# Masks of a top-128 selection read off the scores that sixteen rounds of replacement have taken out

## The chip, the cores and the metric

The kernel runs on one core of a Trainium2 chip. The metric is the device time of one execution in microseconds (us), median of three runs. Engines are named as the profile names them: PE (matrix products), PEld (its weight loads), DVE (VectorE), ACT (ScalarE), POOL (GpSimd), SP (the engine whose queue issues all transfers here, SPq in the rows). Each engine works through its own instructions in order and waits for semaphores of the others.

## The reference

One decoder layer on 512 tokens of width 1024: rmsnorm, one wide projection, two token mixers side by side, a gated merge, a feed-forward block, a last rmsnorm. The first mixer (A) is a mixture of dilated attentions. The second (B) is attention over selected keys, and the selection is what the change touches:

```python
def one_block(args):                      # 128 queries at a time
    causal = key_pos[None, :] <= q_pos[:, None]
    dots = jnp.einsum('bqhd,bsd->bqhs', qi_blk, ki)
    score = jnp.einsum('bqh,bqhs->bqs', wi_blk, jax.nn.relu(dots)) * IDX_SCALE
    score = jnp.where(causal[None], score, -jnp.inf)
    _, sel = lax.top_k(score, topk)       # topk = min(256, T // 4) = 128
    valid = sel <= q_pos[None, :, None]
    ...                                   # softmax over the selected keys only
    return jnp.einsum('bhqk,bqkd->bhqd', p, v_sel)
```

So each query of the blocks 1, 2 and 3 (the tokens from 128 on) attends to the 128 earlier tokens of the highest score; queries of block 0 have at most 128 and take all of them.

## The kernel before, in words

Tokens stand in four blocks of 128. All products are of float32 accuracy: each operand is split into a high and a low part (`whi`/`wlo` for weights, `hTh`/`hTl` for the normalised input), and `mm3` (lines 203 to 205) issues three products. Weights come through `Chunk`: a transfer into `raw` on the SP queue, a copy to `whi` on ACT (line 174), a subtraction to `wlo` on POOL (line 166).

Scores. Before 85 us the scores of mixer B stand in `score[3]`, `score[2]`, `score[1]`, of 512, 384 and 256 columns (one row a query); block 0 needs no selection. A POOL operation (line 872) fills the keys after the query with LOWEST = -3.0e38.

Selection. The generator `topk_ops` (from line 625) searches all three blocks side by side: sixteen times `max` gives the eight largest of each row (line 631), and `match_replace` writes LOWEST over these eight (line 636) in the copy `cur[b]`; after the sixteenth `max` no replacement is made. Then six operations a block turn the 128th value into a mask: count the ties at the threshold among the 128 (line 642), find the ties in the row (644), number them by a scan (646), keep as many as are needed (647), add all that are larger (648), and map 1 and 0 to 0 and -1e30 (649). All of it is on DVE. The mask lies in the tile of the scores, and mixer B's softmax adds it (line 680).

What runs beside it. From 77 us on, the attention of mixer A runs, one `attn_step` after another: score products (`sc`, line 615), softmax (`sm`: DVE line 680, ACT line 681, reciprocal on DVE line 685, scaling on POOL line 686), transposes (`pT`, line 695), split of the transposed probabilities (`pth` on ACT line 699, `ptl` on DVE line 700), value products (`y`, lines 709 to 712), their sum (`A1y`, line 716, with `low` on ACT line 714). Between the steps PE works off a queue of projections, among them `proj` for va (values of mixer A) and `slot` for queries, keys and gates. va is split as well: the high half on ACT (line 564), the low half on DVE (line 565), two tiles a product, and the product's PSUM tile (`acc`, three of them) is free after the second low half. A slot product for keys is copied out by ACT (`raw`, line 490), crossed by two transfers into `sw` (line 493), and rotated on DVE (`z`, lines 497, 500, 501), then split into `kBh` on ACT (458) and `kBl` on DVE (462).

What sets the order. PE's order is as written in the code (a manual schedule). The other engines' orders are made when the program is built, by a scheduler that picks by priority levels: attention at level 2, projections at level 3, the selection at level 4, last. Once built, each engine's order is fixed; an instruction that comes late holds back all behind it on its engine.

Of the kernel before, what the change touches and what calls it, by code (L numbers as in the profile page):

```python
# [11 lines left out]
F32 = mybir.dt.float32  # L12
F32R = mybir.dt.float32r
AF = mybir.ActivationFunctionType
ALU = mybir.AluOpType

P = 128
# [9 lines left out]
TOPK = 128  # L27
EPS = 1e-6
NEG = -1.0e30
LOWEST = -3.0e38  # L30
ATTN_SCALE = HD ** -0.5
IDX_SCALE = (64 ** -0.5) * (8 ** -0.5)

# [5 lines left out]
def hybrid_block(ctx: ExitStack, tc: tile.TileContext, x, norm_mix, w_in, w_up_a, w_up_b, w_out,  # L39
                 norm_ffn, w_gate, w_up, w_down, norm_final, c_rope, c_ropeT, c_mask, out):  # L40
    nc = tc.nc
# [7 lines left out]
    small = ctx.enter_context(tc.tile_pool(name="small", bufs=4))  # L49
    at_stack = ExitStack()  # L50
    wp = ctx.enter_context(tc.tile_pool(name="wp", bufs=1))
    ap = at_stack.enter_context(tc.tile_pool(name="ap", bufs=1))
# [14 lines left out]
    def k2(dt=F32, name="k2"):  # L67
        return kp.tile([P, 512], dt, tag="k2", bufs=K2, name=name)
# [287 lines left out]
    def fill(us):  # L356

        debt[0] += us
        with level(3):
            while queue and debt[0] > 0:  # L360
                run_part()
        if not queue:
            debt[0] = min(debt[0], 0.0)
# [245 lines left out]
    def qk_units(units, name):  # L609

        tiles = [sps(name) for _ in units]
        mms = [qk(t, q, k, half, b, (b + 1) * P) for t, (q, k, half, b) in zip(tiles, units)]
        for i in range(2):
            for m in mms:
                nc.tensor.matmul(*m[i], start=i == 0, stop=i == 1)
        return tiles
# [7 lines left out]
    top, cur = {}, {}  # L624

    def topk_ops():

        for r in range(TOPK // 8):
            for b in (3, 2, 1):
                src = score[b] if r == 0 else cur[b]  # L630
                yield nc.vector.max(top[b][:, 8 * r:8 * r + 8], src[:, :(b + 1) * P])
            if r < TOPK // 8 - 1:
                for b in (3, 2, 1):
                    w = (b + 1) * P
                    src = score[b] if r == 0 else cur[b]
                    yield nc.vector.match_replace(cur[b][:, :w], top[b][:, 8 * r:8 * r + 8], src[:, :w], LOWEST)
        for b in (3, 2, 1):
            w = (b + 1) * P
            thr = top[b][:, TOPK - 1:TOPK]
            need = small.tile([P, 1], F32, name="need")  # L640
            e0 = ap.tile([P, TOPK], F32, tag="e0", bufs=1, name="e0")
            yield nc.vector.tensor_scalar(e0, top[b], thr, None, op0=ALU.is_equal, op1=ALU.add, accum_out=need)
            eq = ap.tile([P, 512], F32, tag="eq", bufs=1, name="eq")[:, :w]
            yield nc.vector.tensor_scalar(eq, score[b][:, :w], thr, None, op0=ALU.is_equal)
            cs = cur[b][:, :w]
            yield nc.vector.tensor_tensor_scan(cs, eq, eq, 0.0, op0=ALU.add, op1=ALU.bypass)
            yield nc.vector.scalar_tensor_tensor(eq, cs, need, eq, op0=ALU.is_le, op1=ALU.mult)
            yield nc.vector.scalar_tensor_tensor(eq, score[b][:, :w], thr, eq, op0=ALU.is_gt, op1=ALU.add)
            yield nc.vector.tensor_scalar(score[b][:, :w], eq, 1.0, -NEG, op0=ALU.subtract, op1=ALU.mult)
            maskb[b] = score[b]  # L650

    topk = []
# [15 lines left out]
    class Head:  # L668
# [6 lines left out]
        def softmax(self, p_, b):  # L675
# [3 lines left out]
            st = small.tile([P, 3], F32, name="st", bufs=8)  # L679
            nc.vector.tensor_tensor_reduce(sm, p_[:, :w], self.mask(b), -ATTN_SCALE, 3.0e38, ALU.add, ALU.min, st[:, 0:1])  # L680
            nc.scalar.activation(sm, sm, AF.Exp, bias=st[:, 0:1], scale=-1.0, accum_out=st[:, 1:2])  # L681
# [172 lines left out]
    score = {}  # L854
    for b in (3, 2, 1):
        w = (b + 1) * P
        score[b] = sc = ap.tile([P, 512], F32, tag="score", bufs=3, name=f"score{b}")
        sp = k2(name="scorep") if PH[0] >= 0 else None
        for hp in range(4):
            for s, p_ in enumerate(qk_units([(idxT[1 + hp], idxT[0], s, b) for s in range(2)], "dots")):  # L860
                h = 2 * hp + s
                rl = ap.tile([P, 512], F32, tag="sm", bufs=4, name="relu")
                nc.scalar.activation(rl[:, :w], p_[:, :w], AF.Relu)
                eng, to = (nc.gpsimd, sp) if h in PH else (nc.vector, sc)
                if h == 0 or h == PH[0]:
                    eng.tensor_scalar(to[:, :w], rl[:, :w], wis[:, b, h:h + 1], 1.0, op0=ALU.mult, op1=ALU.mult)
                else:
                    eng.scalar_tensor_tensor(to[:, :w], rl[:, :w], wis[:, b, h:h + 1], to[:, :w], op0=ALU.mult, op1=ALU.add)
                if sp is not None and h == NH - 1:
                    nc.vector.tensor_tensor(sc[:, :w], sc[:, :w], sp[:, :w], op=ALU.add)  # L870
            fill(DOTF)
        nc.gpsimd.affine_select(out=sc[:, b * P:w], in_=sc[:, b * P:w], compare_op=ALU.is_ge, fill=LOWEST, base=0,
                                pattern=[[-1, P]], channel_multiplier=1)
    drain()
    for b in (3, 2, 1):
        top[b] = const.tile([P, TOPK], F32, name=f"top{b}")
        cur[b] = ap.tile([P, 512], F32, tag="cur", bufs=3, name=f"cur{b}")
    topk.append(topk_ops())

    PLO[0] = PLOA  # L880
# [149 lines left out]
    for f in range(0, NF, 2):  # L1030
# [14 lines left out]
        for j in range(2):  # L1045
# [11 lines left out]
            tag, bufs = (("y", YB) if i >= 2 else ("rp", 2) if i == 1 else ("k2", K2))  # L1057
# [141 lines left out]
def _constants():  # L1199
# [10 lines left out]
    n[d < 0] = 0  # L1210
    mask = np.where(n > 0, np.log(np.maximum(n, 1)) / ATTN_SCALE, NEG).astype(np.float32)
    return tab, tabT, mask
# [24 lines left out]
```

## Time and profile before

| what | before |
|---|---|
| median of three runs | 767.15 us (764.58 to 769.06) |
| the profiled execution | 764.99 us, of which the span from first to last instruction 763.2 |
| PE busy | 733.3 us, 96% of the span |
| DVE busy | 503.4 us, 66% |
| ACT busy | 378.4 us, 50% |
| POOL busy | 258.8 us, 34% |
| mean granted clock of PE | 0.991 |

How to read it: the time of a profiled execution is its span and a little around it. Shares are means over the whole span; a stage of 30 us can have another bound than the mean tells. A row of the trace gives the start (or, in groups, the sum), the duration, the engine, the line of the kernel, and in brackets how long the engine stood idle before it and who released it. PE's products overlap, so the distance between two starts says more than a duration.

### The profile page before, as it was taken

The numbers are of one execution on the slowest core, as the hardware profiler recorded it, in microseconds if no ns is written. First come the engines' busy times: TensorE is split into PE (matmuls) and PEld (weight loads), VectorE is DVE, ScalarE is ACT, GpSimd is POOL, SyncE is SP. The second block draws the span as 40 slices with busy tenths as digits, with TensorE's granted clock in tenths as the row PEclk, the third lists the DMA queues.
The fourth block names the chain that finished last, engine by engine and source line by source line (L and its number), as shares of the span: only waits on it lengthen the run. The fifth ranks groups of instructions, "written<-read, shape, count | busy, mean of one in ns | idle before, by whom it ended". The sixth has DMA issues, their size and how long they took to land.

```text
span 763.2 us, 10914 instructions
## 1 busy us (share of the span) xinstructions
PE 733.3 (96%) x3567; PEld 616.1 (81%) x3567; DVE 503.4 (66%) x1063; ACT 378.4 (50%) x771; POOL 258.8 (34%) x245
## 2 busy tenths in 40 slices
PE   8987998997999999999999999999999999999995
PEld 7976887886888888888887888888888888888874
DVE  5879998999757557848225444344454457877885
ACT  6366656665656666634246333333333334545553
POOL 1653567563554554523222222222222220000043
PEclk9999999999999999999999999999999999999999
DMA  7342243322342212443332343334433452756722
GB/s 266 96 124 70 67 120 91 95 65 70 84 126 70 69 57 69 141 137 105 100 85 69 103 131 110 104 105 131 131 105 104 130 179 84 230 171 212 248 84 110
DMA packets 76280, 88.70 MB, mean 116 GB/s; under 512 B 6256, under 2 KB 57600, under 8 KB 76224
## 3 DMA queue, kind: packets, MB, share of 16 engines
q1 hardware_dynamic: 76224, 88.02, 38.3%
q8 instruction: 28, 0.46, 0.2%
q14 instruction: 28, 0.23, 0.1%
HBM read 79.08 MB, written 5.64 MB: 111 GB/s over the span
## 4 chain that ended last, share of the span: by engine, by line
PE 79%; DVE 13%; ACT 3%; issue 3%; DMA 1%; POOL 1%; SPq 0%; DVEq 0%; ACTq 0%; POOLq 0%
PE u L204 5%; PE u L205 5%; PE u L203 5%; PE g L205 5%; PE g L204 5%; PE g L203 5%; PE o L205 4%; PE o L203 4%; PE o L204 4%; PE gate L203 3%; PE gate L204 3%; PE gate L205 3%; PE x L203 2%; PE x L205 2%; PE x L204 2%
## 5 line engine op out<-in xcount | busy, mean ns | idle before, releaser
L166 POOL TENSOR_TENSOR wlo<-raw,whi 128x512 fp32r<-128x512 f32 (+1 forms) x138 | 183.4, 1339 | 401.8 <-ACT whi L174 398.5
L174 ACT ACTIVATE whi<-raw 128x512 fp32r<-128x512 f32 (+1 forms) x206 | 126.7, 624 | 164.2 <-PE u L205 70.0
L166 DVE TENSOR_TENSOR wlo<-raw,whi 128x512 fp32r<-128x512 f32 x68 | 50.7, 746 | 67.6 <-ACT whi L174 67.1
L205 PE MATMUL g<-h2l,whi 128*128 128x512 f32 x176 | 68.7, 390 | 0.0
L203 PE MATMUL g<-h2h,whi 128*128 128x512 f32 x176 | 68.7, 390 | 0.0
L204 PE MATMUL g<-h2h,wlo 128*128 128x512 f32 x176 | 68.6, 390 | 0.0
L203 PE MATMUL u<-h2h,whi 128*128 128x512 f32 x176 | 68.5, 389 | 0.0
L204 PE MATMUL u<-h2h,wlo 128*128 128x512 f32 x176 | 68.5, 389 | 0.0
L205 PE MATMUL u<-h2l,whi 128*128 128x512 f32 x176 | 68.5, 389 | 0.0
L686 POOL TENSOR_SCALAR sm<-sm,st 128x256 f32<-128x256 f32 (+3 forms) x64 | 40.0, 632 | 60.1 <-DVE st L685 50.8
L203 PE MATMUL gate<-hTh,whi 128*128 128x512 f32 x128 | 51.6, 403 | 0.0
L205 PE MATMUL gate<-hTl,whi 128*128 128x512 f32 x128 | 50.2, 392 | 0.0
L204 PE MATMUL gate<-hTh,wlo 128*128 128x512 f32 x128 | 50.1, 392 | 0.0
L1050 DVE TENSOR_TENSOR u<-u,rb 128x512 f32<-128x512 f32 x22 | 15.2, 691 | 49.0 <-PE u L205 49.0
L681 ACT ACTIVATE sm<-sm,st 128x256 f32<-128x256 f32 (+3 forms) x64 | 35.6, 557 | 23.6 <-DVE st L680 23.5
L203 PE MATMUL slot<-hTh,whi 128*128 128x512 f32 x104 | 42.4, 407 | 1.8 <-DVE va L565 1.1
L203 PE MATMUL proj<-whi,hTh 128*128 128x256 f32 (+1 forms) x128 | 38.3, 301 | 3.7 <-DVE va L565 1.6
L205 PE MATMUL slot<-hTl,whi 128*128 128x512 f32 x104 | 41.6, 400 | 0.0
L204 PE MATMUL slot<-hTh,wlo 128*128 128x512 f32 x104 | 41.4, 398 | 0.0
L203 PEld LDWEIGHTS u<-h2h,whi 128*128 128x128 f32 x176 | 33.0, 188 | 6.9
L204 PEld LDWEIGHTS u<-h2h,wlo 128*128 128x128 f32 x176 | 33.0, 188 | 6.9
L204 PE MATMUL proj<-whi,hTl 128*128 128x256 f32 (+1 forms) x128 | 38.0, 297 | 0.6 <-DVE hTl L315 0.6
(351 smaller groups left out, 1849.1 us busy)
## 6 DMA issues: line engine op xcount, KB each, us to landing
raw<-in_w_in SPq DMA_DIRECT2D x54, 256.0 KB, 3.0
raw<-in_w_gate SPq DMA_DIRECT2D x44, 256.0 KB, 2.8
raw<-in_w_up SPq DMA_DIRECT2D x44, 256.0 KB, 2.9
raw<-in_w_down SPq DMA_DIRECT2D x43, 256.0 KB, 4.2
wraw<-in_w_down SPq DMA_DIRECT2D x28, 256.0 KB, 3.3
x<-in_x SPq DMA_DIRECT2D x16, 256.0 KB, 4.6
raw<-in_w_in SPq DMA_DIRECT2D x32, 128.0 KB, 2.6
raw<-in_w_out SPq DMA_DIRECT2D x16, 256.0 KB, 2.6
```

Of the source, the lines that this page charges most:

```text
L166: eng.tensor_tensor(lo, raw, hi.bitcast(F32), op=ALU.subtract)
L174: nc.scalar.activation(hi, raw, AF.Copy)
L203: nc.tensor.matmul(o, l[0], r[0], start=start, stop=False)
L204: nc.tensor.matmul(o, l[1], r[0], start=False, stop=False)
L205: nc.tensor.matmul(o, l[0], r[1], start=False, stop=stop)
L681: nc.scalar.activation(sm, sm, AF.Exp, bias=st[:, 0:1], scale=-1.0, accum_out=st[:, 1:2])
L686: nc.gpsimd.tensor_scalar(sm, sm, st[:, 2:3], 1.0, op0=ALU.mult, op1=ALU.mult)
L1050: nc.vector.tensor_tensor(u, p_, rb2, op=ALU.mult)
```

## The change

The sixteenth round replaces too, as the fifteen before it. After it every selected score in `cur[b]` is LOWEST and nothing else is, since the keys after the query are now filled with another constant, NEVER = -3.3e38. The mask is read off with one operation a block: not equal to LOWEST gives 1, times NEG = -1e30. The six operations a block and their tiles (`need`, `e0`, `eq`) go.

```diff
+NEVER = -3.3e38
...
-            if r < TOPK // 8 - 1:
-                for b in (3, 2, 1):
-                    w = (b + 1) * P
-                    src = score[b] if r == 0 else cur[b]
-                    yield nc.vector.match_replace(cur[b][:, :w], top[b][:, 8 * r:8 * r + 8], src[:, :w], LOWEST)
+            for b in (3, 2, 1):
+                w = (b + 1) * P
+                src = score[b] if r == 0 else cur[b]
+                yield nc.vector.match_replace(cur[b][:, :w], top[b][:, 8 * r:8 * r + 8], src[:, :w], LOWEST)
         for b in (3, 2, 1):
             w = (b + 1) * P
-            thr = top[b][:, TOPK - 1:TOPK]
-            need = small.tile([P, 1], F32, name="need")
-            e0 = ap.tile([P, TOPK], F32, tag="e0", bufs=1, name="e0")
-            yield nc.vector.tensor_scalar(e0, top[b], thr, None, op0=ALU.is_equal, op1=ALU.add, accum_out=need)
-            eq = ap.tile([P, 512], F32, tag="eq", bufs=1, name="eq")[:, :w]
-            yield nc.vector.tensor_scalar(eq, score[b][:, :w], thr, None, op0=ALU.is_equal)
-            cs = cur[b][:, :w]
-            yield nc.vector.tensor_tensor_scan(cs, eq, eq, 0.0, op0=ALU.add, op1=ALU.bypass)
-            yield nc.vector.scalar_tensor_tensor(eq, cs, need, eq, op0=ALU.is_le, op1=ALU.mult)
-            yield nc.vector.scalar_tensor_tensor(eq, score[b][:, :w], thr, eq, op0=ALU.is_gt, op1=ALU.add)
-            yield nc.vector.tensor_scalar(score[b][:, :w], eq, 1.0, -NEG, op0=ALU.subtract, op1=ALU.mult)
+            yield nc.vector.tensor_scalar(score[b][:, :w], cur[b][:, :w], LOWEST, NEG, op0=ALU.not_equal, op1=ALU.mult)
             maskb[b] = score[b]
...
-        nc.gpsimd.affine_select(out=sc[:, b * P:w], in_=sc[:, b * P:w], compare_op=ALU.is_ge, fill=LOWEST, base=0,
+        nc.gpsimd.affine_select(out=sc[:, b * P:w], in_=sc[:, b * P:w], compare_op=ALU.is_ge, fill=NEVER, base=0,
```

The instruction orders of PE, POOL and SP are the same in both programs. DVE's differs from the end of the sixteenth search to the next softmax but one, ACT's in the place of one va. Line numbers of the changed kernel are smaller by 10 from line 660 on (680 becomes 670), and larger by one before the selection. In the rows, cur_1085, cur_1087, cur_1089 and score_738, score_838, score_958 are the blocks 3, 2, 1.

DVE behind the sixteenth search, before:

```order
L642 TENSOR_SCALAR e_1231,need<-top_1084 128x128
L644 TENSOR_SCALAR eq<-score_738,top_1084 128x512
L680 ISA sm,st<-sc,lc 128x512
L680 ISA st 128x1
L680 ISA sm,st<-sc,lc 128x256
L680 ISA st 128x1
L700 TENSOR_TENSOR ptl<-pT,pth 128x128
L700 TENSOR_TENSOR ptl<-pT,pth 128x3x128
L685 RECIPROCAL st<-st 128x1
L646 SCALAR_TENSOR_TENSOR cur_1085<-eq 128x512
L685 RECIPROCAL st<-st 128x1
L642 TENSOR_SCALAR e_1240,need<-top_1086 128x128
```

and the same place now (from the first reciprocal on):

```order
L675 RECIPROCAL st<-st 128x1
L636 MATCH_REPLACE cur_1087<-top_1086,cur_1087 128x384
L675 RECIPROCAL st<-st 128x1
L636 MATCH_REPLACE cur_1089<-top_1088,cur_1089 128x256
L498 TENSOR_TENSOR z<-raw,ropeT 64x512
L639 TENSOR_SCALAR score_738<-cur_1085 128x512
L639 TENSOR_SCALAR score_838<-cur_1087 128x384
L639 TENSOR_SCALAR score_958<-cur_1089 128x256
L566 SCALAR_TENSOR_TENSOR va_2060<-proj,rs_147,va_2060 128x2x64
L566 SCALAR_TENSOR_TENSOR va_2063<-proj,rs_147,va_2063 128x2x64
```

What moved: of the old operations only three replacements and three masks are left, the masks now stand in one row, and the first two low halves of va follow right behind them.

DVE around the fourth low half of va (the second of va_2084, in the changed program va_2063), before:

```order
L462 TENSOR_TENSOR kBl<-z,kBh 64x512 x2
L685 RECIPROCAL st<-st 128x1 x2
L565 SCALAR_TENSOR_TENSOR va_2084<-proj,rs_147,va_2084 128x2x64
L716 TENSOR_TENSOR A1y<-y,low 64x512
L700 TENSOR_TENSOR ptl<-pT,pth 128x4x128
L700 TENSOR_TENSOR ptl<-pT,pth 128x2x128
L647 SCALAR_TENSOR_TENSOR eq<-cur_1087,need,eq 128x384
```

and now:

```order
L463 TENSOR_TENSOR kBl<-z,kBh 64x512 x2
L675 RECIPROCAL st<-st 128x1 x2
L566 SCALAR_TENSOR_TENSOR va_2060<-proj,rs_147,va_2060 128x2x64
L706 TENSOR_TENSOR A1y<-y,low 64x512
L690 TENSOR_TENSOR ptl<-pT,pth 128x4x128
L690 TENSOR_TENSOR ptl<-pT,pth 128x2x128
L566 SCALAR_TENSOR_TENSOR va_2063<-proj,rs_147,va_2063 128x2x64
```

What moved: it stood ahead of A1y and the two ptl, and stands behind them now; ahead of A1y there is the third one in its place.

ACT at the same place, before:

```order
L564 ACTIVATE va_2084<-proj,rs_147 128x2x64
L564 ACTIVATE va_2081<-proj,rs_147 128x2x64
L458 ACTIVATE kBh<-z 64x512 x2
L564 ACTIVATE va_2084<-proj,rs_147 128x2x64
L681 ACTIVATE sm,st<-sm,st 128x384
L681 ACTIVATE sm,st<-sm,st 128x128
L714 ACTIVATE low<-y 64x512
L699 ACTIVATE pth<-pT 128x4x128
L699 ACTIVATE pth<-pT 128x2x128
L564 ACTIVATE va_2081<-proj,rs_147 128x2x64
```

and now:

```order
L565 ACTIVATE va_2063<-proj,rs_147 128x2x64
L459 ACTIVATE kBh<-z 64x512 x2
L565 ACTIVATE va_2060<-proj,rs_147 128x2x64
L671 ACTIVATE sm,st<-sm,st 128x384
L671 ACTIVATE sm,st<-sm,st 128x128
L704 ACTIVATE low<-y 64x512
L689 ACTIVATE pth<-pT 128x4x128
L689 ACTIVATE pth<-pT 128x2x128
L565 ACTIVATE va_2063<-proj,rs_147 128x2x64
L565 ACTIVATE va_2060<-proj,rs_147 128x2x64
```

What moved: the third and the fourth high half of va each stand one place of va later, the third behind the two kBh, the fourth behind low and the two pth.

## Rows read from the trace of the kernel before

**Rows 1.** Busy time by stretch: start:end, length, busy time (instructions) of each engine, clock
```profile
163.50:193.00 29.50, 24.59 (x157) 21.39 (x155) 28.13 (x66) 14.39 (x38) 14.51 (x14) 1.00 0.31 81
...
200.00:220.00 20.00, 20.00 (x103) 16.90 (x102) 13.56 (x36) 13.74 (x33) 10.65 (x12) 1.00 0.35 89
```

**Rows 2.** The instructions on the mask's tile: durations min/median/max, first to last start
```profile
L680 DVE CUSTOM_DVE_ANT_0 sm<-sc,score x24: 412/556/692, 237.3 to 322.3; 128x512 f32<-128x512 f32 x8, 128x384 f32<-128x384 f32 x8, 128x256 f32<-128x256 f32 x8
...
L649 DVE TENSOR_SCALAR score<-eq x3: 360/428/1264, 171.9 to 186.4; 128x512 f32<-128x512 f32 x1, 128x384 f32<-128x384 f32 x1, 128x256 f32<-128x256 f32 x1
```

**Rows 3.** One group of removed instructions, by line, and the replacements' own line
```profile
L648 DVE SCALAR_TENSOR_TENSOR eq<-score,top,eq 128x512 f32<-128x512 f32 (+2 forms) x3 | 4.4, 1474 | 0.1
...
L636 DVE MATCH_REPLACE8 cur<-top,cur x42: 400/542/681, 79.7 to 162.2; 128x512 f32<-128x512 f32 x14, 128x384 f32<-128x384 f32 x14, 128x256 f32<-128x256 f32 x14
```

**Rows 4.** PE in order of time: start, duration, instruction, idle time before and releaser
```profile
166.66 0.34 PE L615 MATMUL sc<-qk1A20h,qk0A 128*128 128x384 f32 x1
...
168.35 0.27 PE L710 MATMUL y<-pth,va 128*128 128x128 f32 x1
...
173.88 0.36 PE L203 MATMUL proj<-whi,hTh 128*128 128x256 f32 x1 [0.90 <-DVE va L565]
...
178.08 0.47 PE L203 MATMUL slot<-hTh,whi 128*128 128x512 f32 x1 [1.09 <-DVE va L565]
...
187.53 0.22 PE L615 MATMUL sc<-qk1A20h,qk0A 128*128 128x128 f32 x1
189.14 0.44 PE L615 MATMUL sc<-qk1A21h,qk0A 128*128 128x384 f32 x1 [1.39 <-DVE st L680]
...
191.02 0.49 PE L710 MATMUL y<-pth,va 128*128 128x512 f32 x1 [1.15 <-DVE st L685]
...
192.38 0.84 PE L695 MATMUL pT<-ident,sm 128*128 128x128 f32 x6
192.98 0.49 PE L203 MATMUL slot<-hTh,whi 128*128 128x512 f32 x1
```

**Rows 5.** DVE in order of time, from the first count to the last va
```profile
163.88 0.33 DVE L642 TENSOR_SCALAR_CACHE_REDUCE e<-top 128x128 f32<-128x128 f32 x1
...
165.32 0.68 DVE L680 CUSTOM_DVE_ANT_0 sm<-sc,lc 128x512 f32<-128x512 f32 x1
...
167.01 1.20 DVE L646 TENSOR_TENSOR_SCAN cur<-eq 128x512 f32<-128x512 f32 x1
...
168.44 0.81 DVE L497 TENSOR_TENSOR z<-raw,ropeT 64x512 f32<-64x512 f32 x1
...
172.80 0.67 DVE L500 TENSOR_TENSOR sw<-sw,ropeT 64x512 f32<-64x512 f32 x1
...
173.66 0.67 DVE L501 TENSOR_TENSOR z<-z,sw 64x512 f32<-64x512 f32 x1
...
178.63 1.02 DVE L700 TENSOR_TENSOR ptl<-pT,pth 128x512 fp32r<-128x512 f32 x2
...
188.40 0.35 DVE L565 SCALAR_TENSOR_TENSOR va<-proj,rs,va 128x128 fp32r<-128x128 f32 x1 [0.44 <-ACT va L564]
```

**Rows 6.** A tensor_scalar of 512 on DVE and a subtraction on POOL, in order of time
```profile
164.13 1.26 DVE L644 TENSOR_SCALAR eq<-score,top 128x512 f32<-128x512 f32 x1
...
169.57 1.71 POOL L166 TENSOR_TENSOR wlo<-raw,whi 128x512 fp32r<-128x512 f32 x1
```

**Rows 7.** The DMA queue: the two transfers of the crossed rope
```profile
167.86 1.15 SPq L493 DMA_DIRECT2D sw<-raw  x2
```

**Rows 8.** Busy time by stretch, elsewhere: PE's busy time and its granted clock
```profile
62.00:64.00 2.00, 0.31 (x2) 0.31 (x3) 1.93 (x4) 1.47 (x3) 0.00 (x0) 1.00 0.42 108
130.00:132.00 2.00, 0.44 (x2) 0.20 (x2) 2.00 (x7) 1.93 (x4) 2.00 (x3) 0.96 0.16 17
132.00:134.00 2.00, 1.70 (x4) 1.42 (x5) 2.00 (x6) 1.03 (x3) 1.58 (x2) 0.50 0.35 114
134.00:136.00 2.00, 2.00 (x7) 1.58 (x7) 0.97 (x5) 1.98 (x5) 0.00 (x0) 0.68 0.00 0
```

## The prediction

> **What bounds the kernel now.** I read the share of each engine by stretch first, then the instructions of TensorE (PE) and VectorE (DVE) in order of time where the edited lines run, then who sits behind whom on ScalarE (ACT), GpSimd (POOL) and the DMA queue. Over the whole span PE is the bound: from 200 us on a stretch of 20 us is 20.00 us of PE work [rows 1], and the four stretches behind it up to 300 us read the same. There a microsecond of DVE work is worth nothing. The edited lines run from 164 to 188 us, though, and that stretch looks different: of 29.50 us PE is busy 24.59 and DVE 28.13 [rows 1]. So DVE is the bound for these 30 us, and PE pays 4.9 us of idle time there.
>
> The result of the edited lines itself is wanted late: the first softmax that reads a mask starts at 237.3 us, the last mask starts at 186.4 us [rows 2]. Some 50 us of slack mean that an earlier mask releases nobody. What counts is only who queues behind these lines on DVE: softmax, rope and the low halves of va, all in one in-order queue.
>
> PE's waits in the stretch are four: 0.90 us before the fourth proj product and 1.09 us before the next slot product, both for the low half of va (it frees the PSUM tile), 1.39 us in the middle of a score product for a softmax that stood behind the last mask, and 1.15 us before a value product whose probabilities ACT could copy only after that softmax [rows 4].
>
> **The change part by part.** *Removed:* eighteen operations behind the sixteenth round. The largest line alone (is_gt, L648) takes 4.4 us in three pieces [rows 3]; a scan over 512 takes 1.20, a count over 128 takes 0.33 us [rows 5]. *Added:* a sixteenth round of match_replace, by the older rounds 0.68, 0.54 and 0.40 us for the three blocks (largest, middle and smallest duration of the line) [rows 3], and three tensor_scalar, whose nearest rows are those of the final mask line of before, 0.36 to 1.26 us [rows 2]. The fill value of the masked corner changes a constant and nothing else: 0. The temporaries eq and e0 give up nothing that anyone waits for: eq's space is next taken by a head's output more than 100 us later.
>
> The instruction order of PE, POOL and the DMA queue is unchanged, DVE's changes only between the sixteenth search and the softmax of the stage behind, ACT's at one va. So I can walk DVE's new order with the old durations.
>
> *Up to the masks.* Before, the first count starts at 163.88, and the next softmax at 165.32 [rows 5]. Now one match_replace of 0.68 stands between: softmax at 164.6, 0.76 us earlier. From softmax to the straight rope product (z from raw) were 3.12 us (165.32 to 168.44) with the scan and one count in it; about 1.4 us of these go (1.20 and 0.33, less what neighbours overlap), and 0.54 and 0.40 come in. So z starts near 168.44 - 0.76 - 1.4 + 0.94 = 167.2; its input, ACT's copy, is ready 0.76 earlier too (its DMA followed at 167.86 [rows 7], so now 167.1). It takes 0.8 and ends at 168.1.
>
> *The three masks in a row.* Undisturbed they are 0.43 + 0.36 + 0.36 = 1.15 us (the shortest and middle duration of the old mask line [rows 2]). Disturbed, one takes 1.26: a tensor_scalar over 512 that met a subtraction on POOL took 1.26, against 0.43 for the middle case of the mask line [rows 2, 6]. On POOL the subtraction that ran at 169.57 for 1.71 us [rows 6] comes up earlier, since the normalisations ahead of it do, and lands about where the masks now stand; nothing else is queued there until the next softmax. Bounds: masks done at T = 169.2 (none held), 171.9 (three times 1.26). I take one held, 1.26 + 0.36 + 0.36, T = 170.1, because POOL has one operation to hold it with.
> The Trainium skill (SBUF — State Buffer, "Who interferes with whom") says that a DVE operation with one SBUF input outside the two-port modes doesn't meet POOL, and that a tensor_scalar may, the loser being blocked for the whole instruction. The trace agrees so far: no match_replace of before exceeds 0.68 us, while the mask line is three times its shortest once. By the rule one POOL operation can hold one mask only, which gives the sum below; without it all three could be held, and the sum would be 1.1 us.
>
> *A va moves behind.* After the masks come the first two low halves of va. They cannot run back to back: ACT writes the second one's high half only after the first low half (the last such pair shows DVE waiting 0.44 us for it [rows 5]), so 0.35 + 0.44 + 0.35 = 1.1 us, to T + 1.1. Then the crossed rope and its sum, 0.67 + 0.67 = 1.3 [rows 5]: z is complete at T + 2.4. The 0.90 us wait of PE is gone, since the second va ends at 171.2, while PE is still in the third proj product. But in the new order the fourth va, which frees the PSUM tile of PE's next slot product, stands behind A1y and two ptl subtractions on DVE, and behind two pth copies on ACT; before it stood ahead of them. From the end of z (173.66 + 0.67) to the end of those ptl (178.63 + 1.02) passed 5.3 us [rows 5], on ACT nearly all of it (kB, three softmax pieces, low, pth), and none of that is shortened. With the va (0.35) and PE's start (0.15) the slot product begins 5.8 us after z: T + 8.2. That is 178.3 for T = 170.1, where before it began at 178.08 [rows 4]. So the waits of 0.90 and 1.09 are not saved but pushed together into one wait of PE, from 176.1 at the latest (178.08 - 1.09, less the 0.90) to 178.3, 2.2 us or somewhat more. This term is -0.2 us, with bounds +0.7 (T = 169.2) and -2.0 (T = 171.9).
>
> *Behind the slot product.* Here nothing is left on DVE but va and softmax, and PE has some 9.4 us of products (178.08 to 187.53) before the score product that waited until 189.14. So the waits of 1.39 and 1.15 go. From the last score product to the next slot product before: 187.53 to 192.98, 5.45 us. The same row of products without a wait: four score and eight value products 166.66 to 168.35 + 0.06 = 1.75, six transposes 192.38 to 192.98 = 0.6, together 2.35 [rows 4]. Saved: 3.1 us.
>
> *Sum:* 3.1 - 0.2 = 2.9 us, bounds 3.8 and 1.1. From 193 us to the end PE has no idle time to speak of up to 300 us, and its order is the same, so the rest of the kernel moves forward by it. The profiled execution took 764.99 us (span 763.2 and 1.8 around it), 2.2 us under the median of 767.15; I subtract from the median: 767.15 - 2.9 = 764.2.
>
> **Rivals.**
> *A, as summed:* 764.2.
> *B, POOL's subtraction misses the masks:* T = 169.2, slot at 177.4, gain 3.8: 763.3. For it: the two may well come in the other order, and z complete at 171.6 has its transfer landed (it is issued at 167.1, 4.5 us ahead; before it was used 4.9 us after its issue [rows 5, 7]). Against: POOL's operation becomes ready while z runs, just ahead of the masks.
> *C, the longer single wait lets PE's clock fall:* before, PE idle most of 130 to 132 us was followed by half the clock (granted 0.50 in 132 to 134, 0.68 in 134 to 136), which costs 1.0 + 0.64 = 1.6 us; but 62 to 64 us, even emptier, was followed by no fall [rows 8]. The new wait is of that length. Gain 2.9 - 1.6 = 1.3: 765.8.
> *D, slower:* all three masks are held for 1.26 us each, because POOL's normalisations are themselves late; T = 171.9, the slot product at 180.1, a wait of PE of 4.0 us, and the clock falls in it. Gain 1.1 - 1.6 = -0.5: 767.6. It decides from T = 171.4 with a fall of the clock, and from T = 173.0 without. Against it: only one of three masks of before was stretched [rows 2], and POOL has one long operation there.
> *E, it doesn't do what it says:* the waits at 189 and 191 us are put down to DVE, yet ACT works in the same order, and if its weight copies or the transfers behind them are what comes last, PE waits as before: gain -0.2 to 0, 767.2. Against: DVE was late by its own queue there, with no idle of note before 188.40 [rows 1, 5].
>
> **How the numbers follow.** A 0.45, B 0.22, C 0.15, D 0.08, E 0.10. The three runs of before lie from 764.58 to 769.06, so a median of three may itself be off by 1 to 2 us. The range 761.2 to 767.0 reaches from B with that spread to just under D and E. About 0.5% (3.8 us, below 763.3) is what a measurement of this kernel can tell from no change: B gets there in half its cases, A in about four of ten through the spread of the medians, C hardly, so 0.32 faster; slower than 771 would need D and an unlucky median, 0.04; the rest, 0.64, is within.
>
> **What would show it.** Right: DVE's last mask ends near 170 us and DVE has idle time from there; the largest wait of PE in 160 to 195 us stands before the slot product, 2 to 3.5 us long, for va; no wait at the score product and the value product behind it; the slot product at 192.98 starts near 190. Wrong: the slot product starts before 177 (then the va is not what bounds it, and the gain is nearer 6); the waits of 1.39 and 1.15 are still there; masks of 1.26 us each; a granted clock below 1 around 178 us; or PE idle newly between 200 and 300 us, which would say that weights and not DVE set the pace once PE is earlier.

## The result: slower by 0.9%, with the local gain in it

The changed kernel takes 773.89 us (median of 11 runs, 769.57 to 775.86), the kernel before 766.16 beside it; the ratio is 1.009, 95% interval 1.007 to 1.011. Of the 11 runs of before one took 4177 us, which the median leaves out. The forecast was 764.2, and its range ended at 767.0: wrong, and on the other side. The profiled execution of the changed kernel took 775.86 us, span 774.0; the one of before 764.99, span 763.2.

The page's first and fifth part of the changed kernel (busy time of each engine; then the costliest groups: line, operation, count, sum in us, mean of one in ns):

```profile
PE 748.6 (97%) x3567; PEld 618.7 (80%) x3567; DVE 492.6 (64%) x1051; ACT 379.1 (49%) x771; POOL 257.0 (33%) x245
...
L204 PE MATMUL g<-h2h,whi 128*128 128x512 f32 x176 | 69.7, 396 | 0.0
L206 PE MATMUL g<-h2l,whi 128*128 128x512 f32 x176 | 69.7, 396 | 0.0
L205 PE MATMUL g<-h2h,wlo 128*128 128x512 f32 x176 | 69.6, 395 | 0.0
```

DVE lost 10.8 us of work, as the change intends. But PE, with the same 3567 products in the same order, is busy 15.3 us longer. The same groups of before:

```profile
L205 PE MATMUL g<-h2l,whi 128*128 128x512 f32 x176 | 68.7, 390 | 0.0
L203 PE MATMUL g<-h2h,whi 128*128 128x512 f32 x176 | 68.7, 390 | 0.0
L204 PE MATMUL g<-h2h,wlo 128*128 128x512 f32 x176 | 68.6, 390 | 0.0
```

The products of the feed-forward part, hundreds of microseconds behind the edit, are each 6 ns longer in the mean. As a stretch of 200 us in that part (start:end, length, PE busy and count, granted clock, DMA), before and then after:

```profile
420.00:620.00 200.00, 200.00 (x884) 1.00 0.39 122
```

```profile
420.00:620.00 200.00, 200.00 (x858) 1.00 0.37 113
```

PE is busy throughout in both, at a granted clock of 1.00 in both, and does 858 products where it did 884. The share of busy time hides this; the count shows it. Since both programs issue the same products in the same order, the start of the n-th product, counted from 0, says where time is won and lost (worked out from the traces, us; the last two columns are experiments told below):

| product | before | after | after - before | E1 - before | E5 - before |
|---|---|---|---|---|---|
| 800 | 160.45 | 159.64 | -0.81 | -1.21 | -1.20 |
| 1000 | 198.11 | 195.74 | -2.37 | -2.96 | -6.77 |
| 1900 | 378.61 | 378.73 | +0.12 | -2.96 | -6.76 |
| 3200 | 670.70 | 678.61 | +7.91 | -2.97 | -6.76 |
| 3300 | 693.37 | 701.28 | +7.91 | -2.97 | -6.77 |
| 3566 | 755.07 | 765.94 | +10.87 | -0.87 | -4.37 |

What stands in the first row comes from ahead of the edit, mostly from the first 15 us (E1 is 1.38 us ahead at product 50 already); the columns are to be read from row to row. Between products 800 and 1000, where the edit lies, the changed kernel wins 1.6 us. From there to product 3200 it loses 10.3 us, spread over all of that stretch, 0.0066 us a product of 512 columns in the feed-forward part. From 3200 to 3300 the two run alike, 22.67 us each.

What the edit itself did, DVE of the changed kernel in order of time, to be read beside [rows 5]:

```profile
163.14 0.68 DVE L636 MATCH_REPLACE8 cur<-top,cur 128x512 f32<-128x512 f32 x1
163.73 0.68 DVE L670 CUSTOM_DVE_ANT_0 sm<-sc,lc 128x512 f32<-128x512 f32 x1
...
166.39 0.90 DVE L498 TENSOR_TENSOR z<-raw,ropeT 64x512 f32<-64x512 f32 x1
167.22 1.97 DVE L639 TENSOR_SCALAR score<-cur 128x512 f32<-128x512 f32 x3
169.12 0.33 DVE L566 SCALAR_TENSOR_TENSOR va<-proj,rs,va 128x128 fp32r<-128x128 f32 x1
169.89 0.35 DVE L566 SCALAR_TENSOR_TENSOR va<-proj,rs,va 128x128 fp32r<-128x128 f32 x1 [0.43 <-ACT va L565]
170.16 0.67 DVE L501 TENSOR_TENSOR sw<-sw,ropeT 64x512 f32<-64x512 f32 x1
170.86 0.68 DVE L502 TENSOR_TENSOR z<-z,sw 64x512 f32<-64x512 f32 x1
...
175.57 1.02 DVE L690 TENSOR_TENSOR ptl<-pT,pth 128x512 fp32r<-128x512 f32 x2
176.51 0.60 DVE L566 SCALAR_TENSOR_TENSOR va<-proj,rs,va 128x128 fp32r<-128x128 f32 x2
```

The last row begins with the fourth va, behind the ptl. PE waits for it, and the waits behind it are gone; PE in order of time, beside [rows 4]:

```profile
177.00 0.47 PE L204 MATMUL slot<-hTh,whi 128*128 128x512 f32 x1 [2.74 <-DVE va L566]
...
188.16 0.22 PE L616 MATMUL sc<-qk1A20h,qk0A 128*128 128x128 f32 x1
188.22 0.39 PE L616 MATMUL sc<-qk1A21h,qk0A 128*128 128x384 f32 x1
...
188.74 0.40 PE L700 MATMUL y<-pth,va 128*128 128x512 f32 x1
...
190.55 0.48 PE L204 MATMUL slot<-hTh,whi 128*128 128x512 f32 x1
```

And the clock fell after that wait, as in [rows 8] (stretches of 2 us; the number after the five engines is the granted clock):

```profile
174.00:176.00 2.00, 0.26 (x3) 0.05 (x1) 1.57 (x5) 1.95 (x7) 0.93 (x2) 1.00 0.00 0
176.00:178.00 2.00, 1.00 (x4) 0.90 (x5) 1.46 (x5) 1.70 (x6) 1.07 (x1) 0.97 0.00 0
178.00:180.00 2.00, 2.00 (x7) 1.61 (x7) 0.35 (x1) 1.58 (x5) 2.00 (x3) 0.50 0.29 67
180.00:182.00 2.00, 2.00 (x10) 1.69 (x9) 1.58 (x7) 1.24 (x5) 2.00 (x3) 0.68 0.70 197
```

### The profile page after: what moved, and what is told of

It is laid out like the page before. It is cut to its first block, busy times and chain, and to the rows that moved or that the text cites. A ratio compares the mean times of both kernels' runs of the same rounds, so it can differ in the third digit from the quotient of the medians.

```text
span 774.0 us, 10902 instructions
## 1 busy us (share of the span) xinstructions
PE 748.6 (97%) x3567; PEld 618.7 (80%) x3567; DVE 492.6 (64%) x1051; ACT 379.1 (49%) x771; POOL 257.0 (33%) x245
## 4 chain that ended last, share of the span: by engine, by line
PE 78%; DVE 11%; issue 3%; ACT 3%; DMA 3%; POOL 1%; SPq 1%; DVEq 0%; ACTq 0%; POOLq 0%
PE u L205 5%; PE u L204 5%; PE u L206 5%; PE g L206 5%; PE g L205 5%; PE g L204 5%; PE o L206 3%; PE o L205 3%; PE o L204 3%; PE gate L204 3%; PE gate L205 3%; PE gate L206 3%; PE slot L204 2%; PE sc L616 2%; PE slot L206 2%
## 5 line engine op out<-in xcount | busy, mean ns | idle before, releaser
L205 PEld LDWEIGHTS g<-h2h,wlo 128*128 128x128 f32 x176 | 33.1, 188 | 8.0
```

The costliest lines, as they stand in the source:

```text
L205: nc.tensor.matmul(o, l[1], r[0], start=False, stop=False)
```

## The experiments

**What could slow every product.** The diff changes no product, but it removes tiles. `need` was one float a partition in four buffers, 128 bytes with its padding, in the pool `small`; that pool lies in front of the weight pool. In the built program of the changed kernel all `whi` and `wlo` therefore lie 128 bytes lower, while the operands that stream past them in these products (`hTh`, `hTl`, later `h2h`, `h2l`) stayed where they were. Theory 1: the distance in the on-chip memory between weights and streamed operands sets the pace. Theory 2: the pace belongs to the instructions, the clock or the day. Theory 3: the loss is the wait before the slot product and what follows from it.

**E1: the changed kernel, the 128 bytes put back.**

```diff
+    pad = small.tile([P, 32], F32, name="pad", bufs=1)
+    nc.gpsimd.memset(pad, 0.0)
```

> The changed kernel with 128 bytes a partition of unused space in front of the weight buffers (where the four buffers of the removed tile need stood), so that whi, wlo and all tiles behind them lie at the addresses of before; instruction order unchanged but for one memset at the start. Theory 1 (addresses): in the changed kernel the products of 512 columns follow each other every 0.233 us in the feed-forward stage, before every 0.227, because the weights lie 128 bytes lower against the operands that stream past them; here the pace is 0.227 again, and what is left is the local gain: 763 +- 1.5 us, ratio to before 0.993 to 0.999. Theory 2 (the slower pace follows the instructions, the clock or the chip on that day): pace 0.233 and about 773 us. Theory 3 (the loss is the wait of PE before the slot product and the fall of the clock behind it): pace 0.227 or not, but still 770 or more.

Measured: 764.3 us (ratio 0.9973, interval 0.9948 to 0.9997). The pace is that of before, in the costliest groups of its page:

```profile
L207 PE MATMUL g<-h2h,whi 128*128 128x512 f32 x176 | 68.7, 390 | 0.0
```

and in its stretch of 200 us:

```profile
420.00:620.00 200.00, 200.00 (x884) 1.00 0.38 120
```

and the wait of 2.75 us before the slot product is still there (PE in order of time), so theory 3 is not the loss:

```profile
176.59 0.47 PE L207 MATMUL slot<-hTh,whi 128*128 128x512 f32 x1 [2.75 <-DVE va L569]
```

From product 1000 to product 3300 the distance to before is constant to 0.01 us (table above): with the addresses restored nothing of the change acts there. Of the 2.1 us that E1 loses between product 3300 and the end, 1.7 are waits of PE for operands that DVE prepares in the last stage: one of 1.4 and one of 1.5 us, against one of 1.1 before.

**E2: the kernel before, its weights moved 128 bytes down.** No instruction differs from before:

```diff
-            need = small.tile([P, 1], F32, name="need")
+            need = ap.tile([P, 1], F32, tag="need", bufs=4, name="need")
```

> The kernel before with its tile need taken from the pool behind the weights and not from the one in front of them: whi, wlo and what follows lie 128 bytes lower, as in the changed kernel; every instruction and every order is that of before. Theory 1 (addresses): the pace of the feed-forward products goes from 0.227 to 0.233 us and the time to 776 to 780 us (before plus some 2200 products of 512 columns by 0.0066 us, 14 us at most). Theory 2: pace 0.227, 766 us, the same as before. Theory 3: 766 us, since the selection's code is that of before.

Measured: 776.02 us, ratio 1.014 (1.012 to 1.017), 10.1 us more than before, and the slow pace, in the costliest groups of its page and in its stretch of 200 us:

```profile
L205 PE MATMUL g<-h2l,whi 128*128 128x512 f32 x176 | 69.7, 396 | 0.0
```

```profile
420.00:620.00 200.00, 200.00 (x858) 1.00 0.37 114
```

So the slow pace comes without the change, by the address alone, and theory 2 falls.

**E3: the changed kernel, 128 bytes in front of everything** (`pad` in the pool `const` instead of `small`).

> The changed kernel with 128 bytes of unused space in front of everything: weights at the addresses of before, but the streamed operands 128 bytes higher than before, so the distance of the two is that of the changed kernel. If the distance between weights and streamed operand decides, pace 0.233 and 773 us as in the changed kernel. If the weights' own address decides (they lie where they lay before), pace 0.227 and 763 us. If neither, the pace is something third.

Measured: 773.76 us, ratio 1.011 (1.009 to 1.013), the slow pace (858 products in the 200 us). The weights lie at the very addresses of before here, and it doesn't help: the distance decides.

**E4: 64 bytes instead of 128** (`pad` of 16 floats).

> The changed kernel with 64 bytes in front of the weights, so that weights lie 64 bytes lower than before, half way. If only a distance that is a multiple of 256 bytes is fast, the pace is slower than 0.227, perhaps between 0.227 and 0.233; if only the half step of 128 is slow, 0.227. Time between 763 and 774 us accordingly.

Measured: 769.27 us, ratio 1.004 (1.001 to 1.006), a pace in between.

**E5: the changed kernel with the 128 bytes, and the va that had moved behind brought ahead.**

```diff
-                nc.scalar.activation(vh, src, AF.Copy, scale=rs1[:, b:b + 1])
-                defer(1, lambda vl=vl, src=src, vh=vh: nc.vector.scalar_tensor_tensor(
-                    vl, src, rs1[:, b:b + 1], vh.bitcast(F32), op0=ALU.mult, op1=ALU.subtract))
+                with level(1 if c else 3):
+                    nc.scalar.activation(vh, src, AF.Copy, scale=rs1[:, b:b + 1])
+                    nc.vector.scalar_tensor_tensor(vl, src, rs1[:, b:b + 1], vh.bitcast(F32), op0=ALU.mult, op1=ALU.subtract)
```

> The changed kernel with the 128 bytes of the first experiment and with the second half of va (both its high and its low halves) raised above the attention's level, so that the fourth low half stands on DVE between the two kBl again and no longer behind A1y and the two ptl; all else of DVE, PE, POOL and the DMA queue stands as it did. If the moved va is what made PE wait 2.75 us before the slot product, that wait goes (PE was ready at 173.8 us in the first experiment); if that wait brought the fall of the clock that follows it (177.0 us, 3.4 us at half), the fall goes too. Both: 764.3 - 2.75 - 1.7 = 759.9 us; the wait alone: 761.6; a wait that only changes its releaser: 764.

Measured: 760.58 us, ratio 0.9927 (0.9904 to 0.995). This version beats both kernels. The wait shrank to 0.44 us, and the clock did not fall (PE in order of time, then the stretches of 2 us):

```profile
174.28 0.48 PE L207 MATMUL slot<-hTh,whi 128*128 128x512 f32 x1 [0.44 <-DVE st L678]
```

```profile
174.00:176.00 2.00, 1.72 (x8) 1.49 (x9) 1.94 (x6) 1.95 (x7) 1.48 (x2) 1.00 0.00 0
176.00:178.00 2.00, 2.00 (x13) 1.55 (x12) 1.30 (x4) 1.44 (x4) 1.33 (x2) 1.00 0.00 0
178.00:180.00 2.00, 2.00 (x11) 1.63 (x10) 0.36 (x2) 1.54 (x4) 2.00 (x2) 1.00 0.50 123
180.00:182.00 2.00, 2.00 (x10) 1.67 (x9) 1.73 (x7) 1.28 (x4) 2.00 (x3) 1.00 0.69 162
```

Against E1 it gains 3.8 us between products 900 and 1000 and nothing anywhere else up to product 3300: 2.3 us of the wait and, by the difference, 1.5 us of the clock (I had estimated 2.75 and 1.7).

**E6: 128 bytes in front of everything and 128 in front of the weights.**

> The changed kernel with 128 bytes in front of everything and another 128 in front of the weights: both streamed operands and weights lie 128 bytes above their addresses of before, so their distance is that of before. If the distance decides: pace 0.227 us, 764 us. If an address of its own decides: a pace above 0.227.

Measured: 763.3 us, ratio 0.9966 (0.995 to 0.998), pace of before (884). With before, E2 or the changed kernel, and E3, this completes a square: streamed operands at their old place or 128 bytes up, weights likewise; fast where both moved or neither did.

**E7 and E8: 384 and 160 bytes in front of the weights.**

> The changed kernel with 384 bytes in front of the weights: their distance to the streamed operands is 256 bytes more than before. If every distance that is a multiple of 256 is fast: pace 0.227 us, 764 us. If only the distances of before are: 0.229 or more.

> The changed kernel with 160 bytes in front of the weights: 32 bytes more than before. With 64 bytes less than before the pace was 0.2289 us, with 128 less 0.2333. If the loss grows with the distance from the nearest multiple of 256 bytes: 0.2267 to 0.229. If any other distance costs the same: 0.233.

Measured: E7 765.16 us, ratio 0.9977 (0.9953 to 1.0001), pace of before; E8 773.47 us, ratio 1.0095 (1.007 to 1.012), the slow pace. A distance greater by 256 bytes is as good as that of before, and 32 bytes off cost as much as 128 off; so the loss does not grow with the distance from the nearest multiple of 256 (64 off on the other side, in E4, cost a third of it). E8 has the pace of the second of my expectations, but the condition of that one, that any other distance costs the same, fails at E4.

All in one table: addresses (bytes in a partition) of the first streamed operand and the lowest weight buffer as the built programs have them, the second less the first modulo 256, and the mean distance in us between the starts of successive products of 512 columns from 420 to 620 us (E4 and E8 are medians of four and two runs):

| kernel | hTh0 | whi | difference mod 256 | products in 420 to 620 | pace | median |
|---|---|---|---|---|---|---|
| before | 81888 | 124128 | 0 | 884 | 0.2267 | 766.16 |
| after | 81888 | 124000 | 128 | 858 | 0.2333 | 773.89 |
| E1 | 81888 | 124128 | 0 | 884 | 0.2267 | 764.30 |
| E2 | 81888 | 124000 | 128 | 858 | 0.2333 | 776.02 |
| E3 | 82016 | 124128 | 128 | 858 | 0.2333 | 773.76 |
| E4 | 81888 | 124064 | 192 | 875 | 0.2289 | 769.27 |
| E5 | 81888 | 124128 | 0 | 884 | 0.2267 | 760.58 |
| E6 | 82016 | 124256 | 0 | 884 | 0.2267 | 763.30 |
| E7 | 81888 | 124384 | 0 | 884 | 0.2267 | 765.16 |
| E8 | 81888 | 124160 | 32 | 859 | 0.2333 | 773.47 |

The changed kernel holds the same test within itself, in its last stage. There the streamed operand is `whi` or `wlo`, and the held one (the one that PE loads as its weights) is an activation. In products 3165 to 3308 these activations lie in the pools behind the weights (an `a4_5h` at 191584, `whi` at 124000, 67584 = 264 x 256 apart): both moved by the same 128 bytes, and these products run at 0.227 us in the changed kernel too. In products 3093 to 3164, of the same kind, the activations lie in front of the weights and did not move: 0.233 us.

The same products show that the sign counts too, as far as the two kinds can be compared (at 0 and at 128 they run alike). In E4 the weights lie 64 bytes lower than before. Where the weight is held (420 to 620 us) the pace is 0.2289; where the weight is streamed and the held activation did not move (products 3093 to 3164), the held operand less the streamed one is 64 modulo 256 and not 192, and the pace of E4 is 0.2333. In E8 that difference is 32 in the first place and 224 in the second, and the pace is 0.2333 in both.

## Why the prediction was wrong

**The step that failed** is one sentence of "the change part by part": that the removed temporaries "give up nothing that anyone waits for" and are worth 0, and with it the last of the sum, that "the rest of the kernel moves forward by it". I had looked at eq and e0 for waits and for space, had left out `need` altogether, and at none of them as something that holds other tiles in their place. What the runs showed there is a pace of 0.2333 us a product where it had been 0.2267, because the weights behind `need` had moved 128 bytes against the streamed operands. That term is +9.6 us: 773.89 against 764.30 in E1, which differs from the changed kernel in that and one memset at its start (9.0 us by the two ratios, each to the kernel before measured beside it). It outweighs all other terms, and none of my rivals was of its kind. Of what I had said would show the forecast wrong, nothing named it either: PE was not idle between 200 and 300 us, it was slower. (One of these signs did come, the clock below 1 around 178 us; it belongs to rival C, below.)

**The rest of the sum** can be read in E1, and in the changed kernel's own rows up to 190 us. To compare with times of before, add 0.80 us: the replacement of the sixteenth round starts at 163.08 (with the load of its eight values, ahead of the row at 163.14), where before the count started at 163.88.

- Softmax at 164.6: it came at 163.73 + 0.80 = 164.5. The straight product z at 167.2: 166.39 + 0.80 = 167.2.
- Three masks, one of them held, 1.98 us: 1.97 us. That the sum fits so well is luck: the held one took 1.50 us and not 1.26, the free ones 0.34 and 0.28 and not 0.36 each, and they overlap a little. The durations of the line's three instructions tell which (in ns, then their stretch and shapes), and POOL in order of time, below them, has the subtraction beside it:

```profile
L639 DVE TENSOR_SCALAR score<-cur x3: 276/342/1500, 167.2 to 168.9; 128x512 f32<-128x512 f32 x1, 128x384 f32<-128x384 f32 x1, 128x256 f32<-128x256 f32 x1
```

```profile
166.85 1.59 POOL L167 TENSOR_TENSOR wlo<-raw,whi 128x512 fp32r<-128x512 f32 x1
```

 POOL's one operation had begun at 166.85 and ended at 168.44, the first mask ended 0.28 us behind it (167.22 + 1.50 = 168.72), the other two ran free. That is what the rule of the Trainium skill weighed there (SBUF — State Buffer, "Who interferes with whom") says of a tensor_scalar that comes second. No run took POOL's operation away to test it; but of the six tensor_scalar of lines 644 and 649 in the kernel before, the two that began within a POOL operation took 1.26 us each, and the four others 0.35 to 0.43.
- Two va in 1.1 us: from 169.12 to 170.16, 1.04. z complete at 172.5: 171.54 + 0.80 = 172.3.
- The fourth va behind the ptl, the slot product at 178.3, a wait of 2.2 us "or somewhat more": 177.00 + 0.80 = 177.8, a wait of 2.74. Right, and E5 shows that the va's place was the cause: moved ahead, the wait falls to 0.44 us.
- The waits of 1.39 and 1.15 go: right, the last score and value products follow without a wait. From the last score product to the next slot product now 188.16 to 190.55, 2.39 us; predicted 2.35.
- The clock (rival C, to which I gave 0.15): it fell, in the profiled executions of all seven versions in which the wait before the slot product was 2.7 to 3.3 us long (the changed kernel, E1, E3, E4, E6, E7, E8), and it did not in E5, where the wait was 0.44. So C, not A, was the case, and its gain of 1.3 us is mis-sized by little: between products 800 and 1000 E1 gains 1.75. The wait of 2.2 us "or somewhat more" and the falls of [rows 8] called for more than 0.15. A shorter wait does not decide it: the one of 1.47 us near 130 us, behind which the clock fell in the kernel before, stands in E1 too (129.89 us), and there the granted clock stayed at 1.00.
- The last stage: I had read PE's idle time up to 300 us only. In E1's profiled execution it takes back 2.1 us, 1.7 of them in waits: more than the edit gains. The median of E1 is still 1.9 us under 766.16 (2.1 us by the ratio); how the median's gain is made up is not shown. That 764.30 lies next to the forecast of 764.2 is luck: I had taken 2.9 from a median of three that stood 1 us above that of eleven.

So within the 30 us that I walked through, no term but the clock misses by much more than half a microsecond, and the fall of the clock, 1.5 us by E5, is enough for the difference between the 2.9 us of the sum and the 1.75 measured. The loss came from the 480 us behind them, in which I had said that nothing would change.

## What to carry to other kernels

An edit that removes, adds or resizes a tile moves every tile behind it, and that can change the time of instructions that have nothing to do with it: where PE is the bound, look at the addresses of its two operands before and after, not at the diff alone. When PE is 100% busy in both traces, count its products per stretch or compare the starts of the n-th product; the busy share says nothing about pace. And a wait that is removed from a full queue can come up again at the operation that the scheduler pushed back: here one va, worth 3.8 us with the clock that fell behind it.

## What the runs showed of the hardware

- The pace of float32r products of 512 columns depends on the distance in a partition between the held operand and the streamed one. With the held one's address less the streamed one's modulo 256, it is 0.2267 us at 0 (before, E1, E5, E6, E7, and 0.227 in products 3165 to 3308 of the changed kernel), 0.2289 at 192 (E4), and 0.2333 at 128 (after, E2, E3), at 32 and 224 (E8) and at 64 (E4). What in the chip does this is not shown: that the read of the next weights meets the read of the streamed operand would fit, but no run separated the two reads, and the records of the weight loads are as long in the slow kernels as in the fast ones (188 ns). Distances with other remainders and other types were not tried, and narrower products were not compared.
- 128 bytes of unused space are worth 9.6 us of 774 in this kernel, five times what the edit itself gains.
